# Two 1024x1024 projections as seven half products of 2x2 blocks with 512-column matmuls, and the embedding projection in one piece between them

## The chip, the cores and the metric

The kernel runs on one core of one Trainium2 chip, on float32 data. The metric is device time of one launch in microseconds. A core has TensorE (PE; its weight loads are listed as PEld), VectorE (DVE), ScalarE (ACT), GpSimd (POOL) and SyncE (SP), which here issues nearly all DMAs. Each engine takes its instructions in the order of its own queue.

## The reference

A layer takes 1024 prompt rows and 64 sample rows `x` (width 1024) through a recurrent branch A and an attention branch B. What the change touches is the end:

```python
    u = jnp.einsum('bsnw,nwd->bsnd', jnp.stack([ya, yb], axis=2), w_branch)
    gates = jax.nn.sigmoid(jnp.stack([ma, mb], axis=2))
    mix = jnp.sum(gates * u, axis=2) @ w_o
    h = x + rms_norm(mix, g_post)
    ple = jax.nn.sigmoid(h @ w_ple_gate) * (pe @ w_ple_proj)
    h = h + rms_norm(ple, g_ple)
```

`w_o` and `w_ple_gate` are 1024x1024, `w_ple_proj` is 256x1024; `pe` is the embedding, 256 wide.

## The kernel before

Every float32 product is made of three passes. An operand is split into a high part (ACT copies it into the rounded type) and a low part (DVE subtracts the high part from it): `copy_act` and `sub`, helper lines L82 and L85. `three` (L162 to L164) then issues high x high, high x low and low x high into one PSUM accumulator. The 64 sample rows use `passes_half` (L176 to L179): their high and low parts lie side by side in one 128-column operand, and the two halves of the result are added afterwards.

After the attention, PE runs branch A's projection to 1024 channels, then branch B's. In branch B's, `evac_b` multiplies each accumulator by its gate, adds what branch A left in `d_mix`, and splits the sum into `mix` (tiles `mxh`, `mxl`, channels on partitions).

The output projection then goes over four quarters of 256 columns of `w_o` (`quarter` loads and splits one, tiles `wqh`, `wql`). For each quarter it goes over eight blocks of 128 prompt rows and the sample; for each block over eight steps of 128 channels, three matmuls each, of 128x128 against 128x256. Each result is copied to `hs[b]` (tile `h`), ACT squares it, and `post_norm` scales it by the inverse root and adds the residual.

The gate goes block by block. `turn_h` transposes `h` and the embedding together (ten 128x128 transposes) and splits the result (`hth`, `htl`); `gate_q` makes one quarter of the gate, `proj_q` one quarter of the embedding projection (`acc7p`, two steps of 128 channels), and `finish` multiplies, squares, scales and stores. The last block does this quarter by quarter, so that little is left after its last matmul.

The PSUM has eight banks of 512 columns of float32; all accumulators and transposes of these stages take them in turn from one pool of eight, so a product hardly ever waits for a bank to be read. The order of the instructions on each engine is set by a scheduler from the program's order and its own estimates; a section up to the end of branch A is given by hand.

Another, earlier projection of the kernel is already made from sums and differences of 2x2 blocks; its tiles are `quad`, `t3h`, `t4h` and `u`.

Of the kernel before, what the change touches and what calls it, by code (L numbers as in the profile page):

```python
# [7 lines left out]
F32 = mybir.dt.float32  # L8
# [5 lines left out]
P = 128  # L14
D = 1024
# [50 lines left out]
def hybrid_step(tc, a, o):  # L66
# [34 lines left out]
    d_b12 = dram.tile([2, P, 4, HT], F32, name="d_b12")  # L101

# [1429 lines left out]
    for k in range(0, KT - 2, 2):  # L1532
        gate(k)
# [135 lines left out]
    NQ = 4  # L1669
    QW = D // NQ  # L1670
    wq0 = sb("wq0", side="right")
    mxpool = sb("mxpool", side="right")
    p5 = sb("p5")
    mix = [tuple(mxpool.tile([P, T], F32R, name=f"mx{i}{of}") for i in "hl") for of in range(KT)]

    def mix_in(of):
        g = gate_in(p5, d_mb[of])
        m = p5.tile([P, T], F32, name="ma_in", tag="ma_in", bufs=2)
        sp.dma_start(m[:, :], d_mix[of])
        return g, m  # L1680

    def quarter(pl, raws, src, q):
        wh = pl.tile([P, KT, QW], F32R, name="wqh", tag="wqh")
        wl = pl.tile([P, KT, QW], F32R, name="wql", tag="wql")
        for i in range(2):
            ks_ = slice(4 * i, 4 * i + 4)
            raw = raws[i] if raws is raw_half else raws.tile([P, KT * P], F32, name="wraw", tag="wraw", bufs=2)
            raw = raw.rearrange("p (k n) -> p k n", k=4)
            sp.dma_start(raw, src[4 * i * P:(4 * i + 4) * P, q * QW:(q + 1) * QW].rearrange("(k p) n -> p k n", p=P))
            copy_act(wh[:, ks_, :], raw)  # L1690
            sub(dve, wl[:, ks_, :], raw, f(wh[:, ks_, :]))
        return wh, wl

    m_next = mix_in(0)
    wo = []
    for of in range(KT):
        g, ma_ = m_next
        if of + 1 < KT:
            m_next = mix_in(of + 1)

        def evac_b(c, t0, n, z):
            s = wpool.tile([P, GC], F32, name="st")
            c_ = slice(t0, t0 + n)
            dve.tensor_tensor(out=s[:, :n], in0=z, in1=g[:, c_], op=ALU.mult)
# [6 lines left out]
        if of == KT - 1:  # L1711
            wo.append(quarter(wq0, raw_half, a["w_o"], 0))
        run(panel_steps(mm, *w, yb, evac_b))
    p5.close()
    ybpool.close()
    wpool.close()

    B7 = [0, 1, NBLK] + list(range(2, NBLK))  # L1720
    hpool = sb("hpool")
    wq = sb("wq", bufs=3)
    tpool = sb("tpool")
    p6 = sb("p6")
    hs = [hpool.tile([P, D], F32, name=f"h{b}") for b in range(NBLK + 1)]
    ssq = hpool.tile([P, NBLK + 1, NQ], F32, name="ssq")
    pool.memset(ssq[DEC:, NBLK, :], 1.0)
    rs6 = hpool.tile([P, 4, NBLK + 1], F32, name="rs6")
    g_post = hpool.tile([P, D], F32, name="g_post")
    sp.dma_start(g_post[:, :], a["g_post"].partition_broadcast(P))  # L1730
    wo.append(quarter(wq, p6, a["w_o"], 1))
    mxs = p6.tile([P, KT, P], F32R, name="mxs")
    for k in range(KT):
        for i in range(2):
            pool.tensor_copy(mxs[:, k, i * DEC:(i + 1) * DEC], f(mix[k][i][:, SEQ:]))
    ops = {}

    pins = {}

    def load_pin(b):  # L1740
        _, n, t0 = x_src[b]
        pin = pins[b] = tpool.tile([P, PLE], F32, name="pe_in", tag="pe_in", bufs=2)
        sp.dma_start(pin[:n, :], a["p_prompt"][t0:t0 + n, :] if b < NBLK else a["p_sample"])

    def turn_h(b, pl, psum):
        n = x_src[b][1]
        pin = pins.pop(b)
        th = pl.tile([P, 10, P], F32R, name="hth", tag="hth")
        tl = pl.tile([P, 10, P], F32R, name="htl", tag="htl")
        for g in range(3):  # L1750
            ks_ = range(4 * g, min(4 * g + 4, 10))
            tp = psum.tile([P, 4, P], F32, name="tp7", tag="acc")
            for i, k in enumerate(ks_):
                src = hs[b][:n, k * P:(k + 1) * P] if k < KT else pin[:n, (k - KT) * P:(k - KT + 1) * P]
                pe.transpose(tp[:, i, :n], src, ident[:n, :n])
            k_ = slice(ks_[0], ks_[0] + len(ks_))
            t = tp[:, :len(ks_), :n]
            h, l = th[:, k_, :n], (tl[:, k_, :n] if n == P else th[:, k_, DEC:])
            with tc.high_priority(AHEAD):
                copy_act(h, t)  # L1760
                sub(dve, l, t, f(h))
        ops[b] = (th, tl)

    def rstd_post(b0, b1):
        v, y, t, r = (rs6[:, i, b0:b1] for i in range(4))
        dve.tensor_reduce(out=r, in_=ssq[:, b0:b1, :], axis=AX.X, op=ALU.add)
        rstd_of(r, r, 1.0 / D, (v, y, t))
# [3 lines left out]
    def load_res(b, pl):  # L1771
        src, n, _ = x_src[b]
        x = x_res[b] = pl.tile([P, D], F32, name="x6", tag="x6")
        sp.dma_start(x[:n, :], src)

    def post_norm(b):
        n = x_src[b][1]
        hb, x = hs[b][:n, :], x_res.pop(b)
        dve.scalar_tensor_tensor(out=hb, in0=hb, scalar=rs6[:n, 3, b:b + 1], in1=g_post[:n, :],
                                 op0=ALU.mult, op1=ALU.mult)  # L1780
        dve.tensor_tensor(out=hb, in0=hb, in1=x[:n, :], op=ALU.add)

    wg = []
    load_res(0, p6)
    load_pin(B7[0])
    load_pin(B7[1])
    for q in range(NQ):
        if q == 0:
            wo.append(quarter(wq, p6, a["w_o"], 2))
        elif q == 1:  # L1790
            wo.append(quarter(wq, p6, a["w_o"], 3))
            wg.append(quarter(wq0, p6, a["w_ple_gate"], 0))
        else:
            wg.append(quarter(wq, p6, a["w_ple_gate"], q - 1))
        wh, wl = wo[q]
        qc = slice(q * QW, (q + 1) * QW)
        for b in range(NBLK + 1):
            _, n, t0 = x_src[b]
            acc = mm.tile([P, 512], F32, name="acc6", tag="acc")
            pairs = [(wh[:, k, :], wl[:, k, :]) for k in range(KT)]  # L1800
            if n == P:
                passes(acc[:, :QW], [((mix[k][0][:, t0:t0 + n], mix[k][1][:, t0:t0 + n]), pairs[k])
                                     for k in range(KT)])
                dve.tensor_copy(hs[b][:, qc], acc[:, :QW])
            else:
                passes_half(acc[:, :QW], [(mxs[:, k, :], pairs[k]) for k in range(KT)])
                lo = p6.tile([DEC, QW], F32, name="lo6")
                copy_act(lo[:, :], acc[DEC:, :QW])
                dve.tensor_tensor(out=hs[b][:n, qc], in0=acc[:n, :QW], in1=lo[:, :], op=ALU.add)
            jk = p6.tile([P, QW], F32, name="junk", tag="junk", bufs=1)  # L1810
            act.activation(out=jk[:n, :], in_=hs[b][:n, qc], func=AF.Square, accum_out=ssq[:n, b, q:q + 1])
            if q == NQ - 1:
                if b == 1:
                    rstd_post(0, 2)
                    post_norm(0)
                    load_res(1, p6)
                elif b == 4:
                    post_norm(1)
                    turn_h(0, tpool, mm)
    p6.close()  # L1820
    mxpool.close()

    p7 = sb("p7", bufs=2)
    with tc.high_priority(AHEAD):
        wg.append(quarter(wq, p7, a["w_ple_gate"], 3))
    rstd_post(2, NBLK + 1)
    pr_raw = p7.tile([P, 2, D], F32, name="pr_raw", bufs=1)
    wph = p7.tile([P, 2, D], F32R, name="wph", bufs=1)
    wpl = p7.tile([P, 2, D], F32R, name="wpl", bufs=1)
    sp.dma_start(pr_raw[:, :, :], a["w_ple_proj"].rearrange("(k p) n -> p k n", p=P))  # L1830
    copy_act(wph[:, :, :], pr_raw[:, :, :])
    sub(dve, wpl[:, :, :], pr_raw[:, :, :], f(wph[:, :, :]))
    load_res(B7[2], p7)
    g_ple = p7.tile([P, D], F32, name="g_ple", bufs=1)
    sp.dma_start(g_ple[:, :], a["g_ple"].partition_broadcast(P))
    load_res(B7[3], p7)

    def product(b, acc, k0, pairs):
        th, tl = ops[b]
        _, n, _ = x_src[b]  # L1840
        if n == P:
            passes(acc, [((th[:, k0 + k, :], tl[:, k0 + k, :]), w) for k, w in enumerate(pairs)])
            return acc
# [122 lines left out]
```

## Time and profile before

| | |
|---|---|
| time, median of 3 runs | 1485.29 us (1483.45 to 1488.75) |
| profiled execution: span | 1483.9 us; no separate device time is given for it |
| granted TensorE clock, mean | 0.991 |
| PE busy | 1449.2 us, 98% |
| DVE busy | 884.4 us, 60% |
| ACT busy | 691.3 us, 47% |
| POOL busy | 356.5 us, 24% |
| branch B's projection | 1150.2 to 1245.5 us of the span |
| output projection | 1245.5 to 1344.2 us |
| gate and embedding projection | 1344.2 to 1476.1 us |
| after the last matmul | 1476.1 to 1483.9 us |

Busy times are summed over the span. A stretch of the span can be asked for by itself, which gives the busy time of each engine in a stage. In the lists of groups the number after the bar is the busy time of all instructions of the group, then the mean duration of one in ns; a matmul's duration includes a pipeline that the next one overlaps, so its pace is read from the starts of neighbours.

### The profile page before, as it was taken

What the parts mean: (1) busy time and instruction counts of PE and PEld (TensorE: products, weight loads), DVE (VectorE), ACT (ScalarE), POOL (GpSimd) and SP (SyncE); (2) the same over time, 40 slices, a digit from 0 to 9 for tenths busy, and PEclk for the clock granted to TensorE, in tenths of its full rate; (3) what the DMA queues carried; (4) which work ended last, traced back from release to release, by engine and by line L of the source; (5) the groups of instructions that cost most, each with busy time, mean ns of one, the idle gap of its engine ahead of it and who ended that gap; (6) DMA issues with size and microseconds to landing.
All of it is one profiled execution on the core that took longest, in us unless ns stands there. A gap on an engine that the chain in (4) does not pass through costs nothing.

```text
span 1483.9 us, 26363 instructions
## 1 busy us (share of the span) xinstructions
PE 1449.2 (98%) x10117; PEld 1425.4 (96%) x10117; DVE 884.4 (60%) x1531; ACT 691.3 (47%) x1339; POOL 356.5 (24%) x434
## 2 busy tenths in 40 slices
PE   8999999999999999999999999989999999999997
PEld 8899999999999999999899999988999999999997
DVE  5555775664326676666556656999755554337644
ACT  4423444442225666565555536556544333334533
POOL 0012332422322333233223223555322000000001
PEclk9999999999999999999999999999999999999999
DMA  6367555763375756555744332211286534215111
GB/s 202 107 130 106 146 168 169 189 189 94 109 201 147 137 130 152 116 135 130 133 119 112 59 83 44 56 42 39 89 264 226 196 121 149 87 42 171 49 47 44
DMA packets 141099, 182.86 MB, mean 123 GB/s; under 512 B 23173, under 2 KB 111725, under 8 KB 140973
## 3 DMA queue, kind: packets, MB, share of 16 engines
q1 hardware_dynamic: 123292, 155.53, 40.8%
q10 hardware_dynamic: 17680, 25.64, 5.0%
q8 instruction: 80, 1.31, 0.4%
q14 instruction: 47, 0.38, 0.1%
HBM read 122.65 MB, written 58.46 MB: 122 GB/s over the span
## 4 chain that ended last, share of the span: by engine, by line
PE 83%; DVE 8%; ACT 4%; DMA 2%; issue 2%; POOL 1%; SPq 0%; ACTq 0%; DVEq 0%; POOLq 0%
PE quad L785 17%; PE acc L164 13%; PE acc L162 13%; PE acc L163 13%; PE tp L1127 4%; PE pv L1155 3%; PE pv L1157 2%; PE s L1105 2%; PE s L1106 2%; PE vacc L162 1%; PE vacc L163 1%; PE vacc L164 1%; DVE u L1401 1%; PE vacc L456 1%; DMA wv_raw<-in_w_in 1%
## 5 line engine op out<-in xcount | busy, mean ns | idle before, releaser
L164 PE MATMUL acc<-xh,wl 128*128 128x364 f32 (+1 forms) x768 | 253.6, 330 | 6.8 <-DVE wl L85 6.8
L162 PE MATMUL acc<-xh,wh 128*128 128x364 f32 (+1 forms) x768 | 254.5, 331 | 1.6 <-ACT st L82 1.5
L163 PE MATMUL acc<-xl,wh 128*128 128x364 f32 (+1 forms) x768 | 253.5, 330 | 0.0
L164 PEld LDWEIGHTS acc<-xh,wl 128*128 128x128 f32 x768 | 145.8, 190 | 7.4 <-DVE wl L85 7.4
L162 PEld LDWEIGHTS acc<-xh,wh 128*128 128x128 f32 x768 | 146.1, 190 | 2.9 <-ACT st L82 2.2
L163 PEld LDWEIGHTS acc<-xl,wh 128*128 128x128 f32 x768 | 145.7, 190 | 0.5
L85 DVE TENSOR_TENSOR wl<-w_raw,wh 128x1024 fp32r<-128x1024 f32 (+1 forms) x66 | 82.4, 1250 | 56.3 <-ACT wh L82 55.2
L1090 POOL TENSOR_SCALAR pb<-pb,sm 128x896 f32<-128x896 f32 (+1 forms) x64 | 61.8, 966 | 205.2 <-DVE sm L1089 186.7
L1085 DVE CUSTOM_DVE_ANT_0 s<-s,mask 128x1024 f32<-128x1024 f32 (+7 forms) x128 | 95.5, 767 | 25.9 <-PE s L1106 25.5
L82 ACT ACTIVATE wh<-w_raw 128x1024 fp32r<-128x1024 f32 (+1 forms) x66 | 64.4, 977 | 62.4 <-PE quad L785 25.9
L85 DVE TENSOR_TENSOR tl<-tp,th 128x512 fp32r<-128x512 f32 x96 | 65.8, 689 | 37.4 <-ACT th L82 37.4
L785 PE MATMUL quad<-xh,wh 128*128 128x272 f32 x384 | 80.7, 291 | 0.0
L785 PE MATMUL quad<-xl,wh 128*128 128x272 f32 x384 | 79.5, 288 | 0.0
L785 PE MATMUL quad<-xh,wl 128*128 128x272 f32 x384 | 79.4, 288 | 0.0
L1087 ACT ACTIVATE pb<-s,nm 128x896 f32<-128x896 f32 (+1 forms) x64 | 61.1, 955 | 34.0 <-DVE nm L1085 24.7
L82 ACT ACTIVATE th<-tp 128x512 fp32r<-128x512 f32 x96 | 57.0, 597 | 41.2 <-PE tp L1127 37.3
L162 PE MATMUL acc<-wqh,hth 128*128 128x256 f32 x256 | 72.7, 284 | 0.0
L163 PE MATMUL acc<-wql,hth 128*128 128x256 f32 x256 | 72.1, 282 | 0.0
L164 PE MATMUL acc<-wqh,htl 128*128 128x256 f32 x256 | 72.1, 281 | 0.0
L164 PE MATMUL acc<-wqh,mxl 128*128 128x256 f32 x256 | 71.6, 280 | 0.0
L162 PE MATMUL acc<-wqh,mxh 128*128 128x256 f32 x256 | 71.6, 280 | 0.0
L163 PE MATMUL acc<-wql,mxh 128*128 128x256 f32 x256 | 71.5, 279 | 0.0
(548 smaller groups left out, 4265.0 us busy)
## 6 DMA issues: line engine op xcount, KB each, us to landing
w_raw<-in_w_in SPq DMA_DIRECT2D x60, 256.0 KB
q<-d_q SPq DMA_DIRECT2D x48, 256.0 KB
k<-d_k SPq DMA_DIRECT2D x48, 256.0 KB
w_raw<-in_w_branch SPq DMA_DIRECT2D x32, 256.0 KB
w_raw<-in_w_in SPq DMA_DIRECT2D x56, 128.0 KB
wraw<-in_w_in SPq DMA_DIRECT2D x20, 256.0 KB
d_k<-oh ACTq DMA_DIRECT2D x16, 272.0 KB
d_k<-kl SPq DMA_DIRECT2D x16, 272.0 KB
```

Of the source, the lines that this page charges most:

```text
L82: return act.activation(out=out, in_=in_, func=AF.Copy, scale=scale)
L85: return eng.tensor_tensor(out=out, in0=in0, in1=in1, op=ALU.subtract)
L162: pe.matmul(out, ah, bh, start=start, stop=False)
L163: pe.matmul(out, ah, bl, start=False, stop=False)
L164: pe.matmul(out, al, bh, start=False, stop=stop)
L785: pe.matmul(acc[:, c, :CW], l[:, k, :], r[:, k, c * CW:(c + 1) * CW], start=(first and k == 0 and p == 0), stop=(k == 3 and p == 2), skip_ ...
L1085: at = book("D", now[0] + HOP_PE, per(D_MAX, n), lambda: dve.tensor_tensor_reduce(out=s[:, :n], in0=s[:, :n], in1=m, scale=-1.0, scalar=-N ...
L1087: free = book("A", at, per(A_EXP, n), lambda: act.activation(out=pr[:, :n], in_=s[:, :n], func=AF.Exp, scale=-1.0, bias=nm, accum_out=sm))
L1090: return free, book("G", at, per(G_NORM, n), lambda: pool.tensor_scalar(out=pr[:, :n], in0=pr[:, :n], scalar1=sm, scalar2=1.0, op0=ALU.mul ...
L1105: pe.matmul(s[:, c0:c0 + w], t["q1"][:, q0:q0 + P], t["k1"][:, c0:c0 + w], start=True, stop=False)
L1127: pe.transpose(tp[:, o0 + i * P:o0 + (i + 1) * P], pr[par][:, kb * P:(kb + 1) * P], ident[:, :])
L1155: pe.matmul(pv[:, :256], v, tl[:, c], start=(g == 0 and j == 0), stop=False)
```

## The change

The rows are taken in four pairs of 128-row blocks (`PAIRS`). A pair's input is a 2x2 matrix of blocks (two row blocks by two halves of 512 channels), and a weight is a 2x2 matrix of 512x512 blocks. Their product, eight block products in the plain form, is made of seven (`ORDER`): forms of the input (`seven_forms`) against B11, T1, B21, T2, T3, T4 and B22, where T1 to T4 are sums and differences of the weight's blocks. Each product is four steps of 128 channels by three passes, all of 512 columns. Products 0 and 2 go to the accumulator `ta`, 1 and 6 to `tc`, and 3, 4 and 5 to `tb`; between 3 and 4, and 4 and 5, DVE reads `tb` (`u2`, `u3`) while it goes on accumulating. So one projection has 4 x 7 x 12 = 336 matmuls of 512 columns where it had 768 of 256, and 32 for the sample where it had 64. Accumulators come from a pool of six banks, transposes from one of two.

The forms' additions run on POOL, their splits on ACT and DVE, three products ahead of PE (`LEAD`), in a ring of four. The weights' blocks are first copied within DRAM to `d_w` in nine copies of 1 MB (`copy_weights`). The T blocks of `w_o` are formed during branch B's projection (`prepare`) and kept in `d_t`; those of `w_ple_gate` at the end of the output projection (`next_weights`). `evac_b` takes its gate in pieces of 364 columns, adds on POOL, and leaves the mix unsplit (`mx0` to `mx3`, `mx_s`). Between the two projections the embedding projection is made for all blocks (`turn_pe`, `project`, operands `pe_h`, `pe_l`), stored to `d_pp` and reloaded by pairs for the gate. The sample's two halves are handled by `times_half`, `half_sum` and `half_more`; its last gate products come after all pairs. `post_norm`'s residual addition and the multiplication by `g_ple` go to POOL.

```diff
+    def copy_weights(n):
+        dst = d_w[n]
...
+        sp.dma_start(dst.rearrange("p (k n) -> p k n", k=4),
+                     src[i * NW:(i + 1) * NW, j * NW:(j + 1) * NW].rearrange("(k p) n -> p k n", p=P))
...
     for k in range(0, KT - 2, 2):
+        for n in range(3):
+            copy_weights(3 * (k // 2) + n)
...
-            dve.tensor_tensor(out=s[:, :n], in0=s[:, :n], in1=ma_[:, c_], op=ALU.add)
-            copy_act(mix[of][0][:, c_], s[:, :n])
-            sub(dve, mix[of][1][:, c_], s[:, :n], f(mix[of][0][:, c_]))
+            eng = dve if of == KT - 1 else pool
+            for lo, hi, dst in places(of, t0, n):
+                eng.tensor_tensor(out=dst, in0=s[:, lo:hi], in1=m[:, lo:hi], op=ALU.add)
+            gate_ahead()
...
+    psq = ps("q6", bufs=6)
+    pst = ps("t6", bufs=2)
...
+    ORDER = ("B11", "T1", "B21", "T2", "T3", "T4", "B22")
+    W = dict(zip(ORDER, X + Y))
+    for i, name in enumerate(("T2", "T3", "T4")):
+        sp.dma_start(f(W[name][1]), stored(i))
+    sp.dma_start(f(W["B22"][1]), held_w("o", 1, 1))
+
+    def seven_forms(r):
+        (r11, r12), (r21, r22) = r
+        yield form(r11)
+        s1 = tmp("s1", 2).rearrange("p (k n) -> p k n", k=4)
+        pool.tensor_tensor(out=s1, in0=r21, in1=r22, op=ALU.add)
+        yield form(s1)
+        yield form(r12)
+        sub(pool, r21, r11, r21)
+        sub(pool, r11, s1, r11)
+        sub(pool, r12, r12, r11)
+        yield form(r11)
...
+    def times(acc, a_, b_, first):
+        (ah, al), (bh, bl) = a_, b_
+        for k in range(4):
+            for i, (l, r) in enumerate(((ah, bh), (ah, bl), (al, bh))):
+                pe.matmul(acc, l[:, k, :], r[:, k, :], start=(first and k == 0 and i == 0),
+                          stop=(k == 3 and i == 2), skip_group_check=not first)
...
+            acc = getattr(self, ("ta", "tc", "ta", "tb", "tb", "tb", "tc")[i])
+            times(acc, self.ready.popleft(), W[ORDER[i]], i in (0, 1, 3))
...
+            elif i == 3:
+                self.u2 = add("u2", self.tb, self.p1)
+            elif i == 4:
+                self.u3 = add("u3", self.tb, self.p1)
+                self.out(1, 1, self.tc, self.u3)
+            elif i == 5:
+                self.out(1, 0, self.tb, self.p1)
+            elif i == 6:
+                self.out(0, 1, self.tc, self.u2)
...
+    for at in drive(steps6, later={2: 4, 5: 8}):
+        if at == 2:
+            s0, s1_ = bank(), bank()
+            times_half(s0, mxs[:, :4, :], W["B11"], True)
+            half_sum(hs_s[:, NW:], s0)
+            times_half(s0, mxs[:, 4:, :], W["B21"], False)
+            half_sum(hs_s[:, :NW], s0)
...
+            times_half(s1_, mxs[:, :4, :], W["T1"], True)
+            split_slot(W["T2"])
+            split_slot(W["T3"])
...
+        if at > 20:
+            next_weights(at - 21)
...
+    turn_pe(0)
+    for b in range(NBLK + 1):
+        if b < NBLK:
+            turn_pe(b + 1)
+        project(b)
+        if b >= 5:
+            if b == 5:
+                r7 = new_raw(0)
+            turn_h(0, r7, *((0, 0), (1, 0), (1, 1), (0, 1))[b - 5])
+    sp.dma_start(f(xa[1]), stored(3))
+    split_slot(xa)
...
+    for p in range(1, PAIRS):
+        before[7 * p] = turns(p, ((0, 0), (1, 0)))
+        before[7 * p + 1] = turns(p, ((1, 1), (0, 1)))
...
+    s0, s1_ = bank(), bank()
+    g0, g1 = tmp("u2")[:DEC, :], tmp("u3")[:DEC, :]
+    times_half(s0, ths[:, :4, :], W["B11"], True)
+    half_sum(g1, s0)
+    times_half(s1_, ths[:, :4, :], W["T1"], True)
+    times_half(s1_, ths[:, 4:, :], W["B22"], False)
+    half_more(g1, s1_)
+    act.activation(out=g1, in_=g1, func=AF.Sigmoid)
+    weigh(PAIRS, DEC, 0, 1, g1)
+    times_half(s0, ths[:, 4:, :], W["B21"], False)
+    half_sum(g0, s0)
+    act.activation(out=g0, in_=g0, func=AF.Sigmoid)
+    weigh(PAIRS, DEC, 0, 0, g0)
+    finish(PAIRS)
```

The scheduler decides where these instructions stand on each engine. On DVE, at the start of the output projection, this stood before: `h<-acc` copies a finished accumulator, `wql` splits half a quarter of the weights.

```order
L85 TENSOR_TENSOR mxl_13253<-st,mxh_13252 128x360
L1804 COPY h_14077<-acc_14134 128x256
L85 TENSOR_TENSOR wql<-wraw,wqh 128x1024
L1804 COPY h_14078<-acc_14162 128x256
L1804 COPY h_14079<-acc_14190 128x256
```

At the same place after the change: `al` is the low part of a form, `sl3l` and `sl4l` are the low parts of T2 and T3 (each split in two halves), `sl5l` and `sl6l` those of T4 and B22, `hs_s<-q,jk` adds the halves of the sample's product, and `u` is the first drain of `tb`.

```order
L85 TENSOR_TENSOR al<-mx_13251,ah 128x512
L85 TENSOR_TENSOR sl3l<-sl3l,sl3h 128x1024 x2
L85 TENSOR_TENSOR al<-mx_13250,ah 128x512
L85 TENSOR_TENSOR sl4l<-sl4l,sl4h 128x1024 x2
L1851 TENSOR_TENSOR hs_s<-q,jk 64x512
L85 TENSOR_TENSOR sl5l<-sl5l,sl5h 128x1024 x2
L1851 TENSOR_TENSOR hs_s<-q,jk 64x512
L85 TENSOR_TENSOR sl6l<-sl6l,sl6h 128x1024 x2
L85 TENSOR_TENSOR al<-mx_13250,ah 128x512 x3
L1881 TENSOR_TENSOR u_14419<-q,p_14257 128x512
```

The splits of two weight blocks that are loaded after branch B now stand ahead of `hs_s`, after which PE can write that bank again.

The second place is DVE between the two projections. Before, the transposed operands `htl` (of `h` and the embedding together) stood between splits of weights and the norm's steps:

```order
L85 TENSOR_TENSOR wql<-wraw,wqh 128x1024
L85 TENSOR_TENSOR htl<-tp_15289,hth 128x512
L85 TENSOR_TENSOR wql<-wraw,wqh 128x1024
L85 TENSOR_TENSOR htl<-tp_15296,hth 128x512
L85 TENSOR_TENSOR htl<-tp_15303,hth 128x256
```

After the change it is the embedding's low part `pe_l`, of blocks 2 and 3 here, with the forming (`s_`) and splitting (`sl`) of the gate's weights between them:

```order
L85 TENSOR_TENSOR pe_l<-tpp,pe_h 128x256
L85 TENSOR_TENSOR s_14933<-sl4l,s_14932 128x512
L85 TENSOR_TENSOR sl5l<-s_14932,sl5h 128x512
L85 TENSOR_TENSOR sl1l<-sl1l,sl1h 128x1024
L85 TENSOR_TENSOR sl6l<-s_14933,sl6h 128x512
L85 TENSOR_TENSOR sl2l<-s_14932,sl2h 128x512
L85 TENSOR_TENSOR sl4l<-sl4l,sl4h 128x1024
L85 TENSOR_TENSOR s_14945<-sl2l,sl1l 128x512
L85 TENSOR_TENSOR sl3l<-sl3l,sl3h 128x1024
L85 TENSOR_TENSOR s_14946<-sl4l,s_14945 128x512
L85 TENSOR_TENSOR sl5l<-s_14945,sl5h 128x512
L85 TENSOR_TENSOR pe_l<-tpp,pe_h 128x256
```

Ten instructions of the weights came between two operands of the embedding projection.

More of the change, by code (lines that the diff above doesn't have):

```diff
@@ L1667, in hybrid_step @@
     ypool.close()
[L1669 to L1672, printed above, removed]
-    p5 = sb("p5")
[L1674 to L1692, printed above, removed]
@@ L1731, in hybrid_step @@
[L1731 to L1745, printed above, removed]
-        n = x_src[b][1]
[L1747 to L1767, printed above, removed]
-    x_res = {}
[L1771 to L1776, printed above, removed]
-        n = x_src[b][1]
[L1778 to L1781, printed above, removed]
@@ L1833, in hybrid_step @@
[L1833 to L1843, printed above, removed]
-        passes_half(acc, [(th[:, k0 + k, :], w) for k, w in enumerate(pairs)])
-        lo = p7.tile([DEC, QW], F32, name="lo7")
-        copy_act(lo[:, :], acc[DEC:, :])
-        dve.tensor_tensor(out=lo[:, :], in0=acc[:n, :], in1=lo[:, :], op=ALU.add)
-        return lo
@@ new lines, in times, with times_half @@
+    def times(acc, a_, b_, first):
[4 more added lines that the diff above has]
+                          stop=(k == 3 and i == 2), skip_group_check=not first)
+    def times_half(acc, x, b_, first):
+        bh, bl = b_
+        n = bh.shape[1]
+        for k in range(n):
+            two = [(acc[:DEC, :], x[:, k, :DEC], bl[:, k, :]), (acc, x[:, k, :], bh[:, k, :])]
+            if first and k == 0:
+                two.reverse()
+            for i, (out, l, r) in enumerate(two):
+                pe.matmul(out, l, r, start=(first and k == 0 and i == 0),
+                          stop=(k == n - 1 and i == 1), skip_group_check=not first)
@@ new lines, in hybrid_step, with drive, make_to @@
+    LEAD = 3
+    def drive(steps, before={}, later={}):
+        made = 0
+        held = []
+        def make_to(n):
+            nonlocal made
+            while made < min(n, len(steps)):
+                if made in before:
+                    before[made]()
+                steps[made][0].make()
+                made += 1
+        for at, (q, i) in enumerate(steps):
+            make_to(at + 1)
+            q.step(i)
+            make_to(at + 1 + LEAD)
+            if at in later:
+                held.append((later[at], q, i))
+            else:
+                q.drain(i)
+            for w_ in [w_ for w_ in held if w_[0] == at]:
+                w_[1].drain(w_[2])
+            yield at
```

448 lines of the change are left out of this document (313 added, 135 removed).

## The prediction, on record before the run

> **What bounds the kernel now.** First the page: its span, its busy times and the shares of the chain that ended last.
>
> ```profile
> span 1483.9 us, 26363 instructions
> PE 1449.2 (98%) x10117; PEld 1425.4 (96%) x10117; DVE 884.4 (60%) x1531; ACT 691.3 (47%) x1339; POOL 356.5 (24%) x434
> PE 83%; DVE 8%; ACT 4%; DMA 2%; issue 2%; POOL 1%; SPq 0%; ACTq 0%; DVEq 0%; POOLq 0%
> POOL 0012332422322333233223223555322000000001
> ```
>
> TensorE is the bound, and POOL is nearly idle in the last quarter. That is an average, so next the busy times by stage: output projection, gate, tail. The columns after the stretch are its length and the busy time of PE, PEld, DVE, ACT and POOL, then the granted clock and the DMA share.
>
> ```profile
> 1245.50:1344.20 98.70, 98.70 (x845) 98.70 (x844) 38.16 (x64) 33.39 (x91) 3.33 (x17) 1.00 0.30 95
> 1344.20:1476.10 131.90, 131.90 (x1121) 131.67 (x1120) 79.50 (x162) 63.14 (x115) 2.93 (x3) 1.00 0.22 75
> 1476.10:1483.90 7.80, 0.18 (x2) 0.00 (x0) 3.38 (x12) 1.87 (x3) 0.96 (x1) 0.80 0.17 67
> ```
>
> PE has no idle microsecond in the two stages that change. Any wait the new form brings is therefore a loss, and only fewer columns through PE can gain. The tail of 7.8 us has no PE work under it.
>
> **Term 1: the matmuls.** The groups by form give the counts, the timeline the pace (start, duration).
>
> ```profile
> L162 PE MATMUL acc<-wqh,mxh 128*128 128x256 f32 x256 | 71.6, 280 | 0.0
> L162 PE MATMUL acc<-wqh,hth 128*128 128x256 f32 x256 | 72.7, 284 | 0.0
> 1289.82 0.28 PE L162 MATMUL acc<-wqh,mxh 128*128 128x256 f32 x1
> ...
> 1292.09 0.28 PE L164 MATMUL acc<-wqh,mxl 128*128 128x256 f32 x1
> 501.68 0.40 PE L1105 MATMUL s<-k,q 128*128 128x512 f32 x1
> 501.92 0.40 PE L1106 MATMUL s<-k,q 68*128 68x512 f32 x1
> 502.15 0.28 PE L1105 MATMUL s<-k,q 128*128 128x256 f32 x1
> ...
> 502.39 0.60 PE L1127 MATMUL tp<-ident,pb 128*128 128x128 f32 x4
> ```
>
> Each projection has three such groups of 256, so 1536 matmuls of 256 columns. Seven products of eight remove an eighth: the columns of 192 such matmuls. The pace of 256 is 98.70 us / 845 = 0.117 us over the stage (0.1135 in the 20 quoted). A 512 starts the next after 0.24 and 0.23 us, so 0.235: twice 0.117. Width itself brings nothing here, and the gain is 192 x 0.117 = **22.5 us**. If a 512 ran at twice the best pace, 0.227, the 840 of them (672 in products, 64 for the sample, 104 for the embedding) would save 840 x 0.008 = 7 us more; that is the other end. The Trainium skill, page TensorE: Matmul & The Clock Gate, section "Wait — 56ns, not 53.3ns?", prices a matmul at N/2.4 + 2.5 ns, which is 216 ns for 512 columns: by it the change would gain some 16 us more (an estimate); the 117 ns of the 256-column rows stand against it, where the rule gives 109.
>
> **Term 2: the drains.** Products 3, 4 and 5 add into one bank, `tb`. After 3 and after 4, DVE reads that bank (u = tb + p1, 128x512), and PE's next product writes it: PE must wait. The trace has just this once, at the `quad` product.
>
> ```profile
> 158.08 0.41 PE L785 MATMUL quad<-xh,wl 128*128 128x272 f32 x2
> 158.60 0.71 DVE L867 TENSOR_TENSOR u__1642<-quad,p__1608 128x544 f32<-128x544 f32 x1
> 159.36 0.52 PE L785 MATMUL quad<-t3h,wh 128*128 128x272 f32 x2 [0.87 <-DVE u__1642 L867]
> ```
>
> The two start 0.25 us apart by pairs (0.125 each), so the next was due at 158.33 and came at 159.36: 1.03 us a drain. Two a pair and four pairs make 8 in the output projection. In the gate the eight transposes of the next pair stand in PE's order between 4 and 5 of pairs 0 to 2, and the sample's lie near pair 3's 3: about 5 are left. 13 x 1.03 = **13.4 us**. It is less only where PE has other work in between, which its order does not show.
>
> **Term 3: DVE is a queue.** What else stands in it ahead of an operation that PE waits for costs too. The durations:
>
> ```profile
> L85 DVE TENSOR_TENSOR wql<-wraw,wqh 128x1024 fp32r<-128x1024 f32 x14 | 17.1, 1223 | 10.6 <-ACT wqh L82 10.4
> L1779 DVE SCALAR_TENSOR_TENSOR h<-h,rs,g_post 128x1024 f32<-128x1024 f32 x8 | 10.1, 1276 | 0.0
> L85 DVE TENSOR_TENSOR tl<-tp,th 128x512 fp32r<-128x512 f32 x96 | 65.8, 689 | 37.4 <-ACT th L82 37.4
> L82 ACT ACTIVATE wqh<-wraw 128x1024 fp32r<-128x1024 f32 x14 | 14.7, 1053 | 8.7 <-DMA wraw<-in_w_o 8.3 <-DMA wraw<-in_w_ple_gate 0.4
> L82 ACT ACTIVATE th<-tp 128x512 fp32r<-128x512 f32 x96 | 57.0, 597 | 41.2 <-PE tp L1127 37.3 <-ACT st L82 2.4 <-PE pv L1157 1.2
> L1861 DVE TENSOR_TENSOR ple<-acc7p,ple 128x256 f32<-128x256 f32 x32 | 13.1, 421 | 29.9 <-PE acc7p L164 24.5 <-ACT ple L1854 5.3
> 1158.00:1164.00 6.00, 6.00 (x38) 6.00 (x37) 2.71 (x6) 3.14 (x4) 0.00 (x0) 1.00 1.00 382
> ```
>
> (a) Start of the output projection. T2 and T3 are loaded (1 MB each) only once branch B's buffers are free, at 1245.5. At the 382 GB/s of the last row a MB takes 2.7 us, so T3, which follows T2 and needs some 3 us of its own from issue (an estimate, from the last store of term 5), lands after 8 to 9 us; ACT's first half (1.05) and two subtractions (2 x 1.22) end it at 12. Behind these stands `hs_s`, which frees the bank of the sample's second product. PE is there after three products and eight sample matmuls, (36 + 8) x 0.235 = 10.3 us. With the copy and add of `hs_s` itself (0.6 + 0.7) it waits 13.3 - 10.3: 3 us, plus the end of the matmul: **3.5**, and at least the 1.5 of `hs_s` alone.
>
> (b) The embedding projection in one piece. Project(0) needs `pe_l` of block 0, behind pair 3's last add, ACT's square of it and two small steps: 0.2 + 0.69 + 0.8 + 0.4 + 0.42, less the transposes that PE still has (four take 0.60 with their end, so 0.1 or so) = 2.4 us. Between `pe_l` of blocks 2 and 3 DVE's order has ten instructions that form gate weights: seven of 512 (0.69) and three of 1024 (1.22), with its own 0.42 8.9 us; PE has one block, 12 x 0.235 plus transposes = 3.0. It waits 5.9. Between blocks 4 and 5 it is 4.4 against 3.0: 1.3. In sum **9.6**.
>
> (c) Single places: pair 1's u3 behind two `h`-shaped steps of post_norm (1.4 exposed), pair 3's u2 behind the split of the embedding weights (1.6), the gate's first u2 behind that of T4 (0.9): **3.9**.
>
> **Term 4: the clock.** PE after a wait of some length:
>
> ```profile
> 735.43 0.50 PE L1105 MATMUL s<-k,q 128*128 128x512 f32 x1 [2.32 <-ACT pb L1087]
> 159.30:162.70 3.40, 3.34 (x26) 3.34 (x27) 2.98 (x5) 2.38 (x4) 0.79 (x1) 1.00 0.02 5
> 736.80:740.20 3.40, 3.40 (x16) 3.32 (x15) 2.63 (x8) 1.16 (x4) 1.42 (x3) 0.52 0.78 176
> ```
>
> A wait of 2.3 us was followed by 3.4 us at a granted 0.52: 3.4 x 0.48 = 1.6 us lost. The waits of (a) and the two long ones of (b) make three: **4.9**; a drain's 1.03 is taken to bring none, as the granted 1.00 behind the one at 159.36 shows.
>
> **Term 5: the tail.**
>
> ```profile
> 1476.00 0.28 PE L164 MATMUL acc<-wqh,htl 128*128 128x256 f32 x1
> 1476.72 1.28 ACT L137 ACT_TABLE_LOAD   x1
> 1479.05 0.16 DVE L142 TENSOR_TENSOR r_r<-r_y,r_t 128x1 f32<-128x1 f32 x1
> 1479.31 1.41 DVE L1914 SCALAR_TENSOR_TENSOR ple<-junk,r_r,h 128x512 f32<-128x512 f32 x2
> ```
>
> Before, 7.9 us follow the last matmul. Now DVE is still finishing pair 3 for 1 us after it; then come three adds of `half_more` and `half_sum` (2.1), a table load and sigmoid (1.8), two multiplies (1.1), the square (0.8), reduce, table load and root chain (2.8), a 1024-wide step (1.28, where two halves overlapped a store before), and the store, 1483.9 - 1480.72 = 3.2 us. They overlap in part: 13, so **5** more.
>
> **Term 6: the rest.** Nine 1 MB copies of weights within DRAM now stand in SP's queue between the loads of `x_in` at the start.
>
> ```profile
> 0.00:37.00 37.00, 32.98 (x202) 32.05 (x203) 19.79 (x51) 18.51 (x38) 1.60 (x11) 0.95 0.61 203
> 37.00:74.00 37.00, 34.23 (x226) 33.17 (x224) 18.97 (x55) 16.65 (x36) 0.00 (x0) 1.00 0.36 107
> ```
>
> The DMA engines have 14 and 24 us free there. A copy takes 2.7 us by the 382 GB/s row, 5.4 if read and write count apart; nine are 24 to 49 us against 38 free, so 0 to 11 us; I take **2**, since most fit. In branch B the 4 MB of loads delay the mix, but eight banks of 3.5 us or more cover that: 0 (0 to 3). The additions that go to POOL cost nothing by themselves, as it is idle.
>
> Sum: -22.5 + 13.4 + 3.5 + 9.6 + 3.9 + 4.9 + 5 + 2 = +19.8.
>
> **Term 7: POOL beside DVE.** POOL now subtracts, adds and multiplies in these stages. Where both work on SBUF operands the trace shows this:
>
> ```profile
> 151.08 0.69 DVE L85 TENSOR_TENSOR wl<-s,wh 128x512 fp32r<-128x512 f32 x1 [1.94 <-ACT wh L82]
> 155.79 2.34 POOL L85 TENSOR_TENSOR wraw<-wraw 128x512 f32<-128x512 f32 x1
> 156.90 1.77 DVE L85 TENSOR_TENSOR wl<-s,wh 128x512 fp32r<-128x512 f32 x1
> 158.82 1.27 POOL L85 TENSOR_TENSOR s<-wraw,s 128x512 f32<-128x512 f32 x1 [0.69 <-DVE wl L85]
> ```
>
> A subtraction of 0.69 us took 1.77 beside a POOL one, and POOL's took 2.34, alone 1.27: they take turns. The Trainium skill, page SBUF — State Buffer, section "Who interferes with whom", has this as a rule that speaks against the change: a DVE instruction with two SBUF inputs and a GpSimd one that reads SBUF exclude each other; the trace agrees. In the embedding projection I add **3** us for it: three of POOL's 1.27 in the ten-instruction gap, less what they hide behind. So +22.8: a span of 1506.7. The profiled span lies 1.4 under the median of 1485.29, which makes **1508**.
>
> **Rivals.** *The gain outlives the waits* (0.14): PE finds `pe_l` and `hs_s` in time, since the order alone does not say when DVE arrives. For it: DVE is busy 38 of 98.7 us in the output projection. Against it: in-order queues and single banks. Then 13.4, the least of (a) 1.5 and half the tail, 2.5, are left: -22.5 + 17.4 = -5.1, 1480; with half the drains hidden 1473. It decides where the formed weights are done before pair 3 ends.
> *Costs equal the gain* (0.08): drains, (a), tail and half of (c) and no more: -22.5 + 23.9, 1487. The faster 512s of term 1 belong here: the forecast less 7 is 1501, and by the page's rule, 16 less, 1492 (0.05 of the forecast's chance).
> *DVE and POOL in turns become the bound* (0.18). A gate pair holds on DVE seven subtractions and four multiplies of 0.69 and two steps of 1.28, 10.2 us; on POOL four and four of 1.27, 10.2; with five PSUM reads of 0.69 that DVE also does, 23.9 against PE's 7 x 12 x 0.235 = 19.7 plus 2 of transposes. It decides as soon as turns are strict; eight pairs x 2.2 = 18 more, 1526.
> *The copies do not fit* (0.05): 9 us more than I took, 1517.
>
> The forecast itself, 1490 to 1520, has 0.55. The chances go by 0.3% (4.5 us), what a measurement of this kernel can tell from no change: faster 0.14, same 0.08, slower 0.78. The range takes in most of the first rival and the lock, 1477 to 1530.
>
> **What would show it.** Right: PE idle in the two stages and between them, released by DVE at `u2`/`u3`, `hs_s` and `pe_l`, near 13, 3.5 and 10 us; 672 product matmuls at 0.235 apart; clock dips behind the long waits; a tail of 13 us. Wrong: drains covered, `pe_l` on time, or a 512 pace well under 0.235.

## The result and the profile after

The changed kernel takes 1550.9 us (median of 4 runs, 1544.2 to 1559.1) where the kernel before takes 1485.8: a ratio of 1.044, 95% interval 1.0398 to 1.0483. The forecast, 1508 in a range of 1477 to 1530, had the direction and missed the size: 65 us slower, not 23. The profiled execution took 1553.1 us with a span of 1551.4. One run of the version with banks of its own (below), 2332 us at a granted clock of 0.556, is in a slower state and is left out of that version's figures.

The page of the changed kernel: span, busy times, POOL's row of the 40 slices, and the row of the granted clock.

```profile
span 1551.4 us, 24731 instructions
PE 1451.2 (94%) x9085; PEld 1375.1 (89%) x9085; DVE 966.2 (62%) x1540; ACT 729.0 (47%) x1391; POOL 492.9 (32%) x529
...
POOL 0012333332223233323333126553123351443351
PEclk9999999999999999999999999999999989989998
```

PE fell from 98% to 94% of a longer span. POOL, nearly idle in the last ten slices before, now works through all of them, and the clock row has dips there.

The same stages as in the prediction: output projection, embedding projection, gate, tail (length, busy PE, PEld, DVE, ACT, POOL, granted clock, DMA share, GB/s).

```profile
1256.80:1378.20 121.40, 96.54 (x371) 74.09 (x370) 86.97 (x103) 49.60 (x93) 45.54 (x23) 0.89 0.33 121
1378.20:1424.10 45.90, 33.17 (x138) 25.20 (x137) 35.88 (x44) 23.52 (x47) 18.52 (x11) 0.85 0.41 139
1424.10:1536.80 112.70, 97.81 (x429) 76.38 (x427) 79.38 (x105) 60.57 (x113) 45.36 (x32) 0.95 0.24 82
1536.80:1551.40 14.60, 0.23 (x1) 0.00 (x0) 7.18 (x15) 5.85 (x10) 2.47 (x2) 0.60 0.27 90
```

Against the rows of before the kernel is 11.3 us late when the output projection starts (1256.8 for 1245.5). That projection takes 121.4 us for 98.7; embedding and gate 158.6 for 131.9; the tail 14.6 for 7.8. That makes 11.3 + 22.7 + 26.7 + 6.8 = 67.5, all of the span's difference. The forecast had 2, 15.8 and 5 for start, stages and tail; so of the 44.7 us by which the span missed, 33.6 lie in the three stages, 9.3 at the start and 1.8 in the tail.

The waits of PE in these stages, by what ended them (total us, times, longest):

```profile
PE q L1830 <- DVE u L1881: 14.9, 11, 4.0
PE q L1830 <- ACT p L82: 13.3, 4, 3.7
PE q L176 <- DVE pe_l L85: 10.4, 2, 6.5
PE q L1841 <- DVE hs_s L1851: 6.2, 1, 6.2
PE q L1830 <- DVE al L85: 3.7, 1, 3.7
```

With four small ones they come to 52 us. The three stages last 280.0 us. The clock row of the stages loses 0.11 x 121.4 + 0.15 x 45.9 + 0.05 x 112.7 = 26 us. By the trace 12 us at half clock fall into PE's waits, so 6 of the 26 are in the 52 already, and 20 come on top. About 208 us of work at full clock are left, where before had 230.6: the matmuls saved some 23 us, as forecast (22.5). Waits and clock took about three times as much back.

Why DVE and ACT were so late is in the groups of DVE in the same stages (busy, mean ns):

```profile
L85 DVE TENSOR_TENSOR al<-mx,ah 128x512 fp32r<-128x512 f32 x23 | 30.8, 1351 | 4.9 <-ACT ah L82 4.9
L1881 DVE TENSOR_TENSOR u<-q,p 128x512 f32<-128x512 f32 x16 | 11.0, 688 | 28.7 <-PE q L1830 28.7
...
L2106 DVE TENSOR_TENSOR mx<-mx,u 128x512 f32<-128x512 f32 x6 | 7.6, 1262 | 1.5 <-ACT u L2118 1.5
```

All three go through 128x512 once: a subtraction, an addition and a multiplication. `u` reads one operand from PSUM and takes 0.688 us, as ever. The two that read both from SBUF take 1.35 and 1.26, twice as much. The timeline at the start of the output projection shows what they do with POOL, first DVE, then POOL:

```profile
1264.47 3.45 DVE L85 TENSOR_TENSOR al<-mx,ah 128x512 fp32r<-128x512 f32 x2
1267.84 1.77 DVE L85 TENSOR_TENSOR al<-s,ah 128x512 fp32r<-128x512 f32 x1
1269.53 1.77 DVE L85 TENSOR_TENSOR al<-mx,ah 128x512 fp32r<-128x512 f32 x1
```

```profile
1265.76 3.30 POOL L85 TENSOR_TENSOR mx<-mx 128x512 f32<-128x512 f32 x2
1269.01 1.74 POOL L85 TENSOR_TENSOR mx<-s,mx 128x512 f32<-128x512 f32 x1
```

Each one waits for the other's: 1.77 us again and again on DVE, which would be 0.69 alone. The second row of PE's waits, for ACT's copy `p`, is the same thing at one remove, here at the end of the gate (DVE, ACT, PE):

```profile
1508.85 1.75 DVE L2106 TENSOR_TENSOR mx<-mx,u 128x512 f32<-128x512 f32 x1
1510.62 0.63 ACT L1937 ACTIVATE u<-mx 128x512 f32<-128x512 f32 x1 [1.62 <-DVE mx L2106]
1511.25 0.58 ACT L82 ACTIVATE p<-q 128x512 f32<-128x512 f32 x1
1511.88 0.50 PE L1830 MATMUL q<-sl3h,ah 128*128 128x512 f32 x1 [3.71 <-ACT p L82]
```

DVE's multiply, drawn out to 1.75, holds ACT's square; behind the square in ACT's queue stands the copy that frees the bank `ta` for product 2; PE waits 3.7 us for it, and from 1512.4 to 1516.0 the granted clock is 0.53.

### The profile page after: what moved, and what is told of

Its sections match the earlier page's. It is cut to its first block, busy times and chain, and to the rows that moved or that the text cites. A ratio compares the mean times of both kernels' runs of the same rounds, so it can differ in the third digit from the quotient of the medians.

```text
span 1551.4 us, 24731 instructions
## 1 busy us (share of the span) xinstructions
PE 1451.2 (94%) x9085; PEld 1375.1 (89%) x9085; DVE 966.2 (62%) x1540; ACT 729.0 (47%) x1391; POOL 492.9 (32%) x529
## 5 line engine op out<-in xcount | busy, mean ns | idle before, releaser
L85 DVE TENSOR_TENSOR wl<-w_raw,wh 128x1024 fp32r<-128x1024 f32 (+1 forms) x66 | 85.8, 1302 | 64.0 <-ACT wh L82 63.9
L1117 PE MATMUL s<-k,q 128*128 128x256 f32 (+1 forms) x192 | 67.1, 353 | 1.5 <-ACT pb L1099 1.5
L1118 PE MATMUL s<-k,q 68*128 68x256 f32 (+1 forms) x192 | 65.0, 350 | 0.0
L176 PE MATMUL acc<-ybh,wl 128*128 128x364 f32 (+1 forms) x192 | 63.1, 329 | 1.9 <-DVE wl L85 1.9
L1139 PE MATMUL tp<-ident,pb 128*128 128x128 f32 x416 | 63.5, 273 | 0.0
L797 PEld LDWEIGHTS quad<-xh,wh 128*128 128x128 f32 x384 | 60.8, 190 | 2.8 <-ACT p__3338 L82 2.5
L175 PE MATMUL acc<-ybl,wh 128*128 128x364 f32 (+1 forms) x192 | 62.9, 328 | 0.0
```

What stands on the lines that cost most here:

```text
L85: return eng.tensor_tensor(out=out, in0=in0, in1=in1, op=ALU.subtract)
L175: pe.matmul(out, ah, bl, start=False, stop=False)
L176: pe.matmul(out, al, bh, start=False, stop=stop)
L797: pe.matmul(acc[:, c, :CW], l[:, k, :], r[:, k, c * CW:(c + 1) * CW], start=(first and k == 0 and p == 0), stop=(k == 3 and p == 2), skip_ ...
L1117: pe.matmul(s[:, c0:c0 + w], t["q1"][:, q0:q0 + P], t["k1"][:, c0:c0 + w], start=True, stop=False)
L1118: pe.matmul(s[:, c0:c0 + w], t["q2"][:HD + 4, q0:q0 + P], t["k2"][:HD + 4, c0:c0 + w], start=False, stop=True)
```

## The experiments

The theory after the comparison: POOL's work on SBUF takes the place of DVE's, so that DVE, in order, is late for everything PE waits for (*exclusion*). The rival, from the prediction's own steps: the waits come from single banks and from what stands in DVE's queue, and POOL costs little (*queues and banks*).

**POOL's work left out.**

```diff
-        pool.tensor_tensor(out=s1, in0=r21, in1=r22, op=ALU.add)
-        yield form(s1)
+        yield form(r21)
...
-        sub(pool, r21, r11, r21)
-        sub(pool, r11, s1, r11)
-        sub(pool, r12, r12, r11)
...
-        pool.tensor_tensor(out=q, in0=q, in1=g_row[:n, c * NW:(c + 1) * NW], op=ALU.mult)
```

> Leaves out what POOL does in the two projections and between them: the four additions of each pair's forms, the residual's addition, the multiplication by g_ple and two subtractions per step of the gate's weights; all other work stays. Theory of the exclusion (a DVE instruction with two SBUF operands and a POOL instruction take turns): al falls from 1.35 us to 0.69, the waits at the start of the output projection (3.9 and 6.4 us) fall to below 4 together, those for ACT's p copy (14 us, since the square ahead of it waits for a DVE multiply that POOL holds up) nearly vanish, and with them most half-clock windows: 25 to 35 us less, about 1516 to 1526. Theory of queues and single banks alone: DVE has time to spare, 5 us less at most, 1546 or more.

Measured: 1514.2 us (1511.8 to 1518.9; 1.0188 of before, interval 1.0165 to 1.0211), 37 less than the changed kernel. Groups of DVE in its new stages:

```profile
L85 DVE TENSOR_TENSOR al<-mx,ah 128x512 fp32r<-128x512 f32 x24 | 16.3, 686 | 9.2 <-ACT ah L82 9.2
L1876 DVE TENSOR_TENSOR u<-q,p 128x512 f32<-128x512 f32 x16 | 11.0, 689 | 19.3 <-PE q L1825 19.3
```

`al` is back at 0.686 and no wait for `p` is left in the list of waits; the largest are `pe_l` 11.9 us, `u` 9.7 and `hs_s` 3.6. From 1245 us to the end DVE is busy for 153.3 us, where the changed kernel has 212.2: some 59 us of DVE's time went with POOL's work, though DVE itself does the same. That fits exclusion. But the time would also fall if PE and ACT had only waited for POOL's results. The next two bear on this.

**POOL working beside, for nobody.** From the kernel above, POOL does as many instructions on operands at hand, into scratch.

```diff
+        def busy(x):
+            pool.tensor_tensor(out=tmp("s1", 2), in0=f(x[0]).rearrange("p k n -> p (k n)"), in1=g_row[:, :NW], op=ALU.add)
+            return x
...
+        yield busy(form(r12))
+        yield busy(form(r11))
```

> As the kernel in which POOL's work is left out (1514.2), but POOL now does as many instructions of the same sizes on operands at hand, into a scratch tile that nothing reads, at about the places where it worked; the two subtractions per step of the gate's weights stay out. Nothing waits for POOL's results. Exclusion theory: al is back at 1.1 to 1.35 us, and the time at 1533 to 1548. The other reading of that run, that PE and ACT waited for POOL's results (chains of forms 1.3 to 1.9 us a link): 1514 to 1519, as without.

Measured: 1538.6 us (1537.0 to 1541.2; 1.0351, interval 1.0331 to 1.037), 24 us slower than without, though nothing waits for what POOL makes. DVE's groups:

```profile
L85 DVE TENSOR_TENSOR al<-mx,ah 128x512 fp32r<-128x512 f32 x24 | 23.9, 1006 | 13.0 <-ACT ah L82 13.0
L1879 DVE TENSOR_TENSOR u<-q,p 128x512 f32<-128x512 f32 x16 | 10.9, 684 | 13.9 <-PE q L1828 13.9
```

And two rows of PE's waits:

```profile
PE q L1828 <- DVE u L1879: 21.4, 12, 5.0
PE q L1828 <- ACT p L82: 3.3, 3, 1.1
```

`al` is drawn out again, a little under the expected 1.1, and `u`, with its PSUM operand, is not. DVE's busy time rises from 153.3 to 184.4 us with the same instructions. So exclusion is shown for 24 of the 37 us. Its path to PE differs: DVE is late with `u` here (21.4 us, 9.7 without POOL), and ACT's copy `p` costs 3.3 where the changed kernel has 13.3. The other 12 us are not told apart: POOL's scratch work draws DVE out less (31 us of busy time for 59), and in the changed kernel ACT does wait for POOL's results (14.7 us in twelve waits). Even here a few waits hang on POOL, for buffers that it still reads: 6.3 us on ACT, 3.4 on DVE, none listed on PE.

**The same work on DVE.**

```diff
-        sub(pool, r21, r11, r21)
-        sub(pool, r11, s1, r11)
-        sub(pool, r12, r12, r11)
+        sub(dve, r21, r11, r21)
+        sub(dve, r11, s1, r11)
+        sub(dve, r12, r12, r11)
```

and so for `s1`, the residual's addition, the multiplication by `g_ple` and the gate's weights.

> The same POOL instructions done by DVE, nothing left out. They cost DVE 0.69 us per 512 columns and 1.22 per 1024, some 48 x 0.69 + 8 x 1.22 = 43 us; by the exclusion theory POOL now takes about 49 us from DVE (the excess of the DVE groups over their undisturbed durations), so it comes out 5 to 15 us faster: 1536 to 1546. By the theory of queues alone DVE gets 43 us more in its queue ahead of what PE waits for: 15 to 30 us slower, 1566 or more.

Measured: 1516.6 us (1513.2 to 1525.4; 1.022, interval 1.0181 to 1.0259). Nothing is left out, DVE has some 43 us more to do (196.9 us busy from 1245 us on, for 153.3 with the work left out), and the kernel is 34 us faster than the changed one, more than either expectation. The waits of PE in its new stages:

```profile
PE q L1830 <- DVE u L1881: 12.1, 11, 1.9
PE q L176 <- DVE pe_l L85: 8.9, 2, 8.7
PE q L1830 <- DVE rs L146: 3.6, 1, 3.6
PE q L1841 <- DVE hs_s L1851: 2.4, 1, 2.4
```

The 13.3 us for `p` and the 3.7 for `al` are gone. What is left is the prediction's list: drains, `pe_l`, a queue place behind the norm's small steps (`rs`), `hs_s`.

**Banks of their own.**

```diff
-            elif i == 3:
-                self.tb = bank()
+            elif i in (3, 4, 5):
+                self.tb = psb.tile([P, NW], F32, name="b", tag="b")[:, :]
...
-                self.u3 = add("u3", self.tb, self.p1)
+                self.u3 = add("u3", self.tb, self.u2)
```

> Products 3, 4 and 5 get accumulators of their own (two banks in turns; u3 = product 4 + u2, last sum = product 5 + u3: as many DVE additions as before), the sample's first sums move to the two banks of the transposes. Takes away the waits of PE for u2 and u3: 13.1 us in the output projection and 5.4 in the gate by the trace, and the half-clock window behind the longest ones: 18 to 23 us less, 1528 to 1533. If PE then only waits as long at the next place for the same late DVE queue (exclusion theory: DVE is what is late), half of it or less: 1541 to 1545.

Measured: 1532.3 us (median of three runs, 1528.6 to 1540.1; 1.0315, interval 1.0276 to 1.0354), 19 less than the changed kernel and at the upper end of the first expectation, though the runs are spread over 12 us. In this run the gate's first sum of a pair overwrites `u3`, so the gate's other sum is formed from other data; the instructions are the same. The waits:

```profile
PE q L1831 <- ACT p L82: 13.0, 4, 3.7
PE ts L1842 <- DVE hs_s L1852: 7.3, 1, 7.3
PE q L176 <- DVE pe_l L85: 5.4, 3, 2.9
...
PE b L1831 <- DVE u L1882: 1.3, 1, 1.3
```

The drains fall from 14.9 to 1.3 us: they are a matter of banks. The waits that hang on the late DVE stay (`p` 13.0), and that for `hs_s` grows from 6.2 to 7.3.

**Copies in their place.** The nine copies keep their place in the program.

```diff
-        sp.dma_start(dst.rearrange("p (k n) -> p k n", k=4),
+        tc.keep_in_program_order(sp.dma_start(
+            dst.rearrange("p (k n) -> p k n", k=4),
```

> The nine 1 MB copies of weights within DRAM keep their place in the program (branch A's loop) instead of standing in SP's queue at the start. If they are what makes the start later (PE's first matmul of the input projection's main part came at 132.3 us instead of 125.2, and the gap of 5.9 us at 49.8 waits for a row block of x), the start is back at 125 us and the time falls by 7 to 9 us, to about 1542 to 1544. If the later 5 us up to 428 us are theirs too, 1539. If DMA at the start is not the cause: 1551, no change. It may cost up to 3 us where the copies now run.

Measured: 1546.0 us (1543.2 to 1551.1; 1.0402, interval 1.0376 to 1.0427): 5 less by the medians, with intervals that overlap those of the changed kernel. The traces are clearer. The changed kernel (the two stretches of the start, and the matmul that waited):

```profile
0.00:37.00 37.00, 33.29 (x200) 32.52 (x201) 19.52 (x51) 18.38 (x38) 1.58 (x11) 0.95 0.86 292
37.00:74.00 37.00, 29.82 (x182) 29.27 (x181) 15.22 (x44) 13.24 (x29) 0.00 (x0) 0.91 0.81 262
...
49.81 1.51 PE L388 MATMUL tp<-ident,xn 128*128 128x128 f32 x6 [5.78 <-DVE xn L372]
```

With the copies late:

```profile
0.00:37.00 37.00, 33.04 (x195) 32.10 (x195) 19.48 (x51) 17.59 (x36) 1.58 (x11) 0.91 0.58 203
37.00:74.00 37.00, 34.79 (x227) 33.71 (x227) 17.50 (x52) 16.77 (x37) 0.00 (x0) 1.00 0.35 107
```

The DMA engines' share falls from 0.86 and 0.81 to that of before, and PE's busy time in the second stretch rises by 5 us: the copies are what made a row block of `x` late. Compared by the starts of the same matmuls, PE is 7.6 us behind the kernel before at 122 us in the changed kernel and 1.5 with the copies late. In this profiled execution (1551.1 us, the longest of the four) nearly all of that is lost again by another wait (3.1 us up to 145.9 us, with a half-clock window behind); the later versions with late copies, whose traces lack that wait, keep it (1.1 us behind at 162 us in the next one, 7.7 in the changed kernel).

**Three together**: copies late, POOL's work on DVE, own banks.

> Three edits together: copies in their place, POOL's additions on DVE, products 3, 4 and 5 in banks of their own. The trace with POOL's work on DVE still has 11.7 us of waits for u2 and u3 in the output projection, 5.8 in the gate, and one half-clock window behind the longest. If single banks are what makes them, they go: from that kernel's 1516.6, 17.5 + 1.6 less, and 5 for the copies (measured alone), so 1492. If DVE, now 43 us fuller, is what is late, the waits come back at other places: 1500 to 1508.

Measured: 1486.2 us (10 runs, 1481.1 to 1489.6; 0.9991, interval 0.9977 to 1.0006): as fast as before, and better than either expectation. The waits add up to 11.7 us: the largest 3.3 for `rs`, 2.8 for `hs_s`, 2.4 for the gate's first `ah`, 1.9 for `pe_l`.

**And the order on DVE.** The splits of T2 to B22 behind the sample's half sums, and

```diff
+        with tc.high_priority(AHEAD):
+            copy_act(h[:, :, :n], tp[:, :2, :n])
+            sub(dve, (l[:, :, :] if n == P else h[:, :, DEC:]), tp[:, :2, :n], f(h[:, :, :n]))
```

> The same, and on DVE the splits of T2, T3, T4 and B22 stand behind the sample's half sums, and the embedding's copy and subtraction (pe_h, pe_l) are taken by the scheduler ahead of the forming of the gate's weights. If the order in DVE's queue is what PE waits for there (2.6 us at the start of the output projection, 0.8 + 8.8 in the embedding, about 5 us lost to the half clock behind), 9 to 12 us less than without: about 1481. If DVE has simply too much to do between the projections, the wait moves to the gate's first pair: within 4 us of the run without.

Measured: 1488.2 us (10 runs; 1.0015, interval 0.9996 to 1.0034): nothing gained. The wait for `pe_l` is gone, and that for the gate's first `ah` has grown from 2.4 to 4.0; `hs_s` still costs 2.6, now behind POOL's former additions in DVE's queue. Between the projections DVE is about as full as PE (27.6 and 28.4 us busy of 29.3), so putting one operand first there only moved the wait to the next one.

**Time between.** The sample's second half product two products later, the norm of pairs 0 to 2 two products later, the sample's gate products ahead of the last two of pair 3:

```diff
+        elif at == 4:
+            times_half(s0, mxs[:, 4:, :], W["B21"], False)
+            half_sum(hs_s[:, :NW], s0)
...
-            post_norm(0)
+        elif at == 11:
+            post_norm(0)
```

> From the run with the queue reordered (1488.2): the sample's second half product goes two products later, so that its half sum has time; each pair's norm is asked for two products after the pair's last one instead of at once, so that DVE does not stand waiting for ACT's root; the sample's gate products go before the last two products of pair 3 instead of behind them. If the waits left there (2.8 us for hs_s, 3.5 behind the rs chain, 1.6 us of half clock behind each, and a tail of 13.6 us) are matters of order, 2.8 + 3.5 + 3.2 + 2 = 11 us less: 1477, the first version below the kernel before. If they are DVE's total load again, they come back elsewhere: 1484 to 1490.

Measured: 1480.9 us (10 runs, 1479.0 to 1482.9; 0.9967, interval 0.9957 to 0.9977), between the two expectations, and the only version faster than before, by a third of a per cent. Its stages, and its one long wait:

```profile
1254.20:1340.10 85.90, 84.57 (x368) 67.67 (x367) 75.09 (x126) 48.98 (x91) 0.00 (x0) 1.00 0.44 162
1340.10:1369.60 29.50, 28.52 (x137) 22.30 (x136) 27.74 (x48) 22.62 (x44) 0.00 (x0) 1.00 0.63 226
1369.60:1466.90 97.30, 93.03 (x428) 74.67 (x426) 81.44 (x139) 60.95 (x114) 0.00 (x0) 0.98 0.30 101
1466.90:1481.20 14.30, 0.00 (x0) 0.00 (x0) 8.64 (x23) 3.88 (x10) 0.00 (x0) 0.61 0.29 92
```

```profile
PE q L1832 <- ACT ah L82: 3.7, 1, 3.7
```

The waits for `hs_s` and `rs` are gone: they were a matter of order. That for the gate's first `ah` stays. The output projection is down to 85.9 us from the 98.7 of before. The three stages, 212.7 us for 230.6, now show the gain; 6.5 of it go in the tail (14.3 for 7.8) and 8.7 ahead of the output projection. The tail did not get shorter: pair 3's chain is as long as the sample's was.

**Width alone.** From the three-together version, every 512-column matmul of the products as two of 256.

```diff
+                for c in (slice(0, NW // 2), slice(NW // 2, NW)):
+                    pe.matmul(acc[:, c], l[:, k, :], r[:, k, c], start=(first and k == 0 and i == 0 and c.start == 0),
```

> The version at 1486.2 (copies in place, POOL's work on DVE, own banks), with every 512-column matmul of the products issued as two of 256. By the prediction width is worth nothing: a 512 takes 0.229 us in that version's trace and two of 256 take 0.227 to 0.234, so 672 products give -1 to +4 us: 1485 to 1490. If a matmul has a cost of its own that the wider form saves, 20 ns each would show as 13 us: 1499.

Measured: 1496.4 us (1493.8 to 1499.7; 1.0072, interval 1.005 to 1.0094), 10 more than with 512. Its timeline in the gate (two matmuls a row), then that of the version with 512 columns:

```profile
1440.17 0.40 PE L1833 MATMUL q<-sl3h,ah 128*128 128x256 f32 x2
1440.41 0.40 PE L1833 MATMUL q<-sl3l,ah 128*128 128x256 f32 x2
```

```profile
1440.05 0.39 PE L1832 MATMUL b<-sl0h,al 128*128 128x512 f32 x1
1440.27 0.39 PE L1832 MATMUL b<-sl0h,ah 128*128 128x512 f32 x1
1440.50 0.39 PE L1832 MATMUL b<-sl0l,ah 128*128 128x512 f32 x1
1440.73 0.39 PE L1832 MATMUL b<-sl0h,al 128*128 128x512 f32 x1
```

0.240 us for two of 256, 0.227 for one of 512: 13 ns, or 9 us in 672 products. That is nearer to the expectation of a cost of its own. The time alone is no proof, though: this run's embedding stage is 9 us longer by waits (`pe_l` 6.3 us for 1.9) while its output projection is as long as with 512 and its gate 0.6 us longer, each against fewer waits or half-clock windows. The pace in the trace is the better measure. Over all neighbours at full clock in the new stages it is 0.228 to 0.229 us for 512 columns in the changed kernel and its variants with 512 and 0.120 for 256 in this run; in the kernel before the 256s are 0.118 apart. Against that kernel width is worth 8 ns in 236, not 13.

## Why the prediction was wrong in size

*Right: what a wait costs and where.* Without POOL's work the prediction's sum stood at +19.8, 1505; the kernel without it measured 1514.2, and the difference is the start (12 us late before the output projection instead of 2). That its three stages come within 2 us of the sum is in part luck: the waits for `u` and `rs` are 11.0 us there for 17.3 forecast, that for `pe_l` 11.9 for 9.6. The single terms, measured without POOL's interference: waits for `u` and the queue places, 17.3 forecast, 15.7 in the kernel with POOL's work on DVE (12.1 + 3.6); `hs_s` 3.5 forecast, 2.4; `pe_l` 9.6 forecast, 8.9, though in one wait of 8.7. Tail 13 forecast, 14.6.

*Wrong: term 7.* The prediction had the row (a subtraction of 0.69 us taking 1.77 beside POOL), named the rule, and then priced it at 3 us, "three of POOL's 1.27 in the ten-instruction gap". It kept the pricing to the one place it was looking at. The runs show 34 to 37 us in the medians: 24 of them come back by POOL merely working beside, and are the exclusion's; the other 12 may in part be waits for POOL's results. In "DVE and POOL in turns become the bound" it was a rival at 0.18 and 1526, and even there the price was only that of throughput (23.9 us of turns against 21.7 of PE). The measured price is one of delay: `al` is late, ACT's square is late behind a DVE multiply, the copy `p` behind the square, and PE waits at the bank. That chain over ACT, 13.3 us in the changed kernel, the prediction did not have at all.

*Wrong: term 4.* Three half-clock windows were forecast, 4.9 us. In the changed kernel eight waits of 3.5 to 6.5 us and a shorter one have half clock behind them, and the stages lost 26 us by the granted clock, 20 of them on top of the waits' 52; in the spread version, with one long wait left, the three stages are at 1.00, 1.00 and 0.98. Part of this is the price of the exclusion, counted above in the medians.

*Wrong: term 6.* The copies were given 2 us out of a range of 0 to 11. They cost some 6 to 7: PE waited 5.8 us for a row block of `x`, a half-clock window followed, and PE was 7.6 us behind instead of about 1. Another 4 to 6 us are lost near 300 us in the changed kernel and all variants but the one with two 256s, also with the copies late: PE waits 2.3 to 2.8 us for a copy of ACT's. Ahead of that copy ACT stood idle for 7.2 us in the changed kernel, by the profile for a DMA (3.2 before, 3.7 with two 256s). Why that transfer came later stays open.

*Small: term 1.* Width does bring something, 8 ns in 236. The gain was some 23 us in the changed kernel and about 26 in the versions with few waits (230.6 us less the 204 that remain without waits and clock): between the 22.5 and the "other end" of 7 more. The rule of the Trainium skill that the prediction cites (page TensorE: Matmul & The Clock Gate, section "Wait — 56ns, not 53.3ns?"), 216 ns for 512 columns, is not reached: the median is 227.

## What to carry to other kernels

An engine that is idle on average isn't free help: POOL takes 1.27 us for what DVE does in 0.69, and beside it DVE's own work with both operands in SBUF stands still (0.69 became up to 1.77). Price such a move by the delay it puts on an in-order queue that the bound engine waits for, link by link, and not by busy time; and where one PSUM bank is read and written in turns, count banks before counting matmuls. If PE is the bound without a gap, each gap costs itself and, from two to three microseconds on, mostly a stretch of half clock: in the eleven traces, from 30 us on, one followed all 62 gaps of PE over 3 us and 27 of the 39 between 2 and 3.

## What was not expected of the hardware

Moving 43 us of work from POOL to DVE made the kernel 34 us faster, and leaving it out altogether only 2.4 more (1514.2 for 1516.6). The exclusion also meets an instruction with few elements: the scalar step `rs` on 128x2 took a mean of 0.77 us beside POOL:

```profile
L146 DVE TENSOR_SCALAR rs<-rs 128x2 f32<-128x2 f32 x8 | 6.2, 771 | 0.3
```

Such a step took about 0.17 in the kernel before, 0.168 with POOL's work left out, and 0.40 again with POOL working beside for nobody.
